# A hybrid decoder trunk on one core: k and three quarters of the gate's operand turned by VectorE in 32x32 blocks that their stores put in place

## The chip, the cores and the metric

One Trainium2 chip, one of its cores. The metric is the device time of one execution in microseconds (us), lower is better. Times of the kernel before are the median of 3 runs; the profile is of one execution more. In the profile PE is TensorE (matmuls), PEld its weight loads, DVE is VectorE, ACT is ScalarE, POOL is GpSimd, and SP is SyncE, whose queue issues almost all DMAs.

## The reference, cut to what matters

One layer of a decoder trunk on 1024 tokens of width 1024, in float32. A combined projection gives, among others, q, k, v, decay gates, and the inputs of a gated short convolution. Branch A is gated linear attention in 4 heads (key width 128, value width 256). Two branches are merged, projected, and added to x; then comes a gate on the sum:

```python
k_in = k * jnp.exp(-b)
k_dec = k * jnp.exp(b_last - b)
a = jnp.where(causal, jnp.einsum('nbhid,nbhjd->nbhij', q_in, k_in), 0.0)
...
def step(state, xs):
    q_n, k_n, v_n, d_n = xs
    o_n = jnp.einsum('bhcd,bhdv->bhcv', q_n, state)
    state = d_n[..., None] * state + jnp.einsum('bhcd,bhcv->bhdv', k_n, v_n)
...
x = x + jnp.einsum('bsd,de->bse', merged, w_out[i])
ple_gate = jax.nn.sigmoid(jnp.einsum('bsd,de->bse', rms_norm(x, norm_ple_g[i]), w_ple_gate[i]))
x = x + ple_gate * jnp.einsum('bsq,qd->bsd', p[i], w_ple_proj[i])
```

Two operands matter here. The state update multiplies k_dec, with time on the partitions, by v; k is made with its 128 key channels on the partitions, so it has to be turned. The gate's product needs x (after the sum) with channels on the partitions; the sum is made with tokens on the partitions, so it has to be turned too.

## The kernel before, in words

**Products.** Every float32 operand is split into a high and a low part of a faster type (`split`: ACT copies the high part, DVE subtracts), and a product is three matmuls, hi by hi, hi by lo and lo by hi (`mm3`). Large products are cut in quarters in Strassen's manner: seven products (k = 0 to 6) of 512x512 by 512x256 or the like instead of eight. A `Cell` is one such product's column block; its seven products run on up to three banks of PSUM, X, V and Y, each product as 12 matmuls of 512 columns. `Cell.run` holds the order: products 2, 4 and 6 all accumulate into Y, and what stands in Y after 2 and after 4 is read by ACT or DVE before the next goes on. The split operand blocks lie in a ring of 8 (`RING`), so an operand can be split up to some seven products ahead, and raw blocks are loaded further ahead (`run_groups`).

**Stages by time in the span.** Start, position embedding and first gate products (to 72 us); v (to 148); z_a (to 234); q and k (234 to 310); the convolution's inputs (to 615); attention woven between the merge gates' products (615 to 746); y_c and y_a (774 to 926); out (926 to about 1008), in four cells out0 to out3 of 256 tokens each, run in pairs; the gate, four cells gt0 to gt3, gt0 and gt1 as a pair and gt2 and gt3 in an order of their own (`CLOSE`), to the end. Cells out0 to out3 and gt0 to gt3 are the groups 0 to 3.

**k.** `k_cons` takes each of 8 k tiles (4 heads, 2 halves of the sequence; 128 channels by 512 times), multiplies it by decays into `kk` (128 x 4 x 256: in each of 4 blocks of times, 128 columns for the scores and 128 for the state), and stores the 256 columns with one DMA into columns 384 to 640 of a row block of the DRAM tensor `qkd`. In attention (`attend`), 32 steps (4 heads, 8 blocks of 128 times) load such rows as `qkl` (128 x 640). In `step_a` PE makes the scores and transposes the last 128 columns of `qkl` into PSUM, `read_a` splits that transpose into `keh` and `kel`, and in the next step PE multiplies it by v (`step_s`). The last block of each head has no state to update, so 28 steps have the transpose. All matmuls of a step are one bundle, which PE runs without other work between.

**The gate's operand.** In `make_out`, a finished tile of x (128 tokens x 512 columns; 4 groups, 2 row blocks i, 2 halves j: 16 tiles) is handed to `finish`, which stores it, weaves in a `flip` two ticks later, and squares it for the norm. `flip` transposes four 128x128 pieces on PE into one PSUM tile `pt_g`, ACT copies that into `gr` (3 buffers), and one DMA stores it into `gd`. The gate cells load their raw blocks from `gd` (`gt0raw` to `gt3raw`); a group's loads are free to start once its four flips have been emitted.

**The order of the work** is not written by hand. Every call is noted in a `Flow`, which keeps dependencies by blocks of `GRAIN` columns of a buffer, gives each operation a cost, works out due times back from the end (`set_dues`), and then orders all engines' instructions with a model of the engines and of the DMA pipe (`put_in_order`). The main products of PE keep their program order; PE's transposes and attention bundles are side work that the planner puts between them. The instructions are emitted in that order, and each engine runs its own in order. A DMA's size for the planner is its bytes, 4 for each element.

Since one line of code (line 520) emits everything, the profile tells instructions apart by the names of their tiles, and the buffer numbers are left out.

Of the kernel before, what the change touches and what calls it, by code (L numbers as in the profile page):

```python
# [9 lines left out]
F32 = mybir.dt.float32  # L10
# [6 lines left out]
P = 128  # L17
# [25 lines left out]


PE, DVE, ACT, POOL, SP = range(5)
GRAIN = 64
TABLE = {AF.Exp: 1, AF.Ln: 2, AF.Sigmoid: 3}


class View:  # L50
# [81 lines left out]
    def place(self):  # L132
        real = self.buf.get()
        if self.dtype != self.buf.dtype:
            real = real.bitcast(self.dtype)
        a, b = self.rows
        return bass.AP(tensor=real.tensor, offset=real.offset + a * self.buf.size + self.off,
                       ap=[[self.buf.size, b - a]] + [[s, n] for s, n in self.dims])


class Buffer:
# [105 lines left out]
class Flow:  # L247
# [12 lines left out]
    def note(self, engine, op, call, args, kw):  # L260
        views = [a for a in args if isinstance(a, View) or hasattr(a, "ap")]
        views += [a for k, a in kw.items() if k not in ("out", "accum_out") and (isinstance(a, View) or hasattr(a, "ap"))]
        outs, ins = ([kw["out"]], views) if "out" in kw else (views[:1], views[1:])
        if kw.get("accum_out") is not None:
            outs.append(kw["accum_out"])
        o = Op()
        o.n, o.engine, o.call, o.args, o.kw = len(self.ops), engine, call, args, kw
        o.side, o.table, o.bytes, o.bufs, o.hurry = self.side, 0, 0, [], self.hurry
        label = lambda v: v.buf.name if isinstance(v, View) else "in"
        o.name = f"{label(outs[0])}<-{','.join(label(v) for v in ins)}"  # L270
        shape = outs[0].shape
        n = 1
        for d in shape[1:]:
            n *= d
        o.lat = 0.15
        if op == "dma_start":
            o.cost, o.bytes = 0.4, shape[0] * n * 4
            o.lat = 2.0 + o.bytes / 250e3
        elif engine == PE:
            o.cost, o.lat = n / 2400 + 0.0134, 0.22  # L280
            if op == "transpose" or args[1].dtype == F32:
                o.cost = 0.11 if op == "transpose" else 0.22
            elif args[1].shape[0] < P:
                o.cost = 0.42
        elif engine == DVE:
            psum = any(isinstance(v, View) and v.buf.pool.name == "ps" for v in outs + ins)
            o.cost = 0.07 + n * (0.00055 if op in ("tensor_scalar", "tensor_copy") and not psum else 0.00104)
            if op in ("scalar_tensor_tensor", "tensor_scalar"):
                o.cost += 0.06
            if op == "tensor_tensor_scan":  # L290
                o.cost = 0.05 + n * 0.0021
        elif engine == ACT:
            o.cost = 0.10 + n * 0.000833 + (0.1 if "accum_out" in kw else 0.0) + (0.08 if len(ins) > 1 else 0.0)
            o.table = TABLE.get(args[2] if len(args) > 2 else None, 0)
        elif engine == POOL:
            o.cost = 0.1 + n * 0.001 if op == "memset" else 0.35 + 0.25 * n
        preds = {}

        def behind(p):
            if p is not None and p != o.n:  # L300
                q = self.ops[p]
                lat = q.lat
                if q.engine == engine and not q.bytes:
                    lat = 0.0 if engine == PE else 0.08
                preds[p] = max(preds.get(p, 0.0), lat)

        for v in ins:
            if isinstance(v, View):
                for b in v.blocks():
                    e = v.buf.memory.setdefault(b, [None, []])  # L310
                    behind(e[0])
                    e[1].append(o.n)
        for v in outs:
            if isinstance(v, View):
                for b in v.blocks():
                    e = v.buf.memory.setdefault(b, [None, []])
                    for p in [e[0]] + e[1]:
                        behind(p)
                    e[0], e[1] = o.n, []
                if engine == PE:  # L320
                    behind(v.buf.group)
                    v.buf.group = o.n
                for pool in v.buf.pool.instead:
                    for old in pool.buffers:
                        for p in old.users:
                            behind(p)
        for v in outs + ins:
            if isinstance(v, View) and v.buf not in o.bufs:
                if v.buf.index is None:
                    v.buf.index = len(v.buf.tag.buffers)  # L330
                    v.buf.tag.buffers.append(v.buf)
                o.bufs.append(v.buf)
                v.buf.users.append(o.n)
        o.preds, o.succs = preds, []
        for p in preds:
            self.ops[p].succs.append(o.n)
        self.ops.append(o)
        if engine == PE and not o.side:
            self.main.append(o)
        if self.bundle is not None and engine == PE:  # L340
            self.bundle.append(o)
# [195 lines left out]
def kernel(  # L537
# [56 lines left out]
    def dram(name, *shape):  # L594
        return dr.tile([P, *shape], F32, name=name)
# [11 lines left out]
    mcd = [[dram(f"mcd{k}_{i}", HALF) for i in range(2)] for k in range(8)]  # L607
    md = [dram(f"md{i}", 2, 2, 2, 4, P) for i in range(2)]
    x2d = [dram(f"x2d{b}", D) for b in range(8)]
    gd = [[dram(f"gd{p}_{q}", 2, 4, P) for q in range(2)] for p in range(4)]  # L610
    wtd = [[dram(f"wtd{w}_{n}", 4, 512) for n in range(4 + 3 * w)] for w in range(2)]

    load = nc.sync.dma_start
# [693 lines left out]
    with phase("qk", [ph["za"]]) as qp:  # L1307
# [35 lines left out]
        def k_cons(hp):  # L1343

            def cons(i, j, src):
                h = 2 * hp + j
                nm = f"{h}_{i}"
                c4 = get_c(h, i, "k")
                kk = qp.tile([P, NP, 4, CH], F32, tag="kk", name=f"kk{nm}", bufs=2)
                dc = dcs[:, h, i]  # L1350
                tt(kk[:, :, 0:4:3, :], c4, c4[:, :, :, CH - 1:CH].to_broadcast([P, NP, 2, CH]), op=ALU.subtract)
                ex(kk[:, :, 0:4:3, :], kk[:, :, 0:4:3, :], 1.0)
                ex(kk[:, :, 1, :], c4[:, :, 1, :], 1.0)
                k4 = src.rearrange("p (n c t) -> p n c t", c=2, t=CH)
                tt(kk[:, :, 0, :], k4[:, :, 0, :], kk[:, :, 0, :], op=ALU.mult)
                tt(kk[:, :, 1:4:2, :], k4[:, :, 1:2, :].to_broadcast([P, NP, 2, CH]), kk[:, :, 1:4:2, :],
                   op=ALU.mult)
                tt(kk[:, :, 2, :], kk[:, :, 0, :], dc[:, :, 1:2].to_broadcast([P, NP, CH]), op=ALU.mult)
                store(qkd[h][i][:, :, 3 * P:5 * P], kk.rearrange("p n s t -> p n (s t)"))
            return cons  # L1360

        for hp in range(2):
# [82 lines left out]
    def attend(hp, ap, every):  # L1445
# [21 lines left out]
        def step_a(it, X):  # L1467
            pr, h = its[it]
            qk = f(ins[it][0])
            mm(X[:, 0:P], qk[:, 3 * P:4 * P], qk[:, 2 * P:3 * P], start=True, stop=True)  # L1470
            if pr < 2 * NP - 1:
                transpose(X[:, P:2 * P], qk[:, 4 * P:5 * P])

        def read_a(it, X):
            pr, h = its[it]
            nm = f"{h}_{pr}"
            a = aTf[it % 2]
            nc.vector.copy_predicated(a, trim, X[:, 0:P])
            ke = None
            if pr < 2 * NP - 1:  # L1480
                ke = (ap.tile([P, P], F32R, tag="keh", name=f"keh{nm}", bufs=2),
                      ap.tile([P, P], F32R, tag="kel", name=f"kel{nm}", bufs=2))
                split(*ke, X[:, P:2 * P])
            aT = (ap.tile([P, P], F32R, tag="aTh", name=f"aTh{nm}", bufs=2),
                  ap.tile([P, P], F32R, tag="aTl", name=f"aTl{nm}", bufs=2))
            split(*aT, a)
            scores[it] = aT, ke
# [178 lines left out]
    with phase("late", [ph["sw"], ep]) as lp:  # L1666
        flipped, rgate, both = set(), {}, [None, None]

        def make_out(p, cell):
# [16 lines left out]
                    ms.append(sm.tile([P, 2], F32, tag="ms2", name=f"ms2_{p}_{i}", bufs=4))  # L1686

            def flip(i, j):
                pt = pso.tile([P, 4, P], F32, tag="o", name=f"pt_g{p}_{i}_{j}", bufs=2)
                for k in range(4):  # L1690
                    transpose(pt[:, k, :], xt[i][j][:, k * P:(k + 1) * P])
                g = lp.tile([P, 4, P], F32, tag="gr", name=f"gr{p}_{i}_{j}", bufs=3)
                nc.scalar.copy(g, pt)
                store(gd[p][j][:, i], g)
                yield 1
                flipped.add((p, i, j))

# [21 lines left out]

        for p in range(4):  # L1720
            make_out(p, outs[p])
        gts = [Cell(f"gt{p}", "A", [gd[p][n // 2][:, n % 2] for n in range(4)], gres, None) for p in range(4)]
        for p, c in enumerate(gts):
            c.ready = lambda k, p=p: {(p, i, j) for i in range(2) for j in range(2)} <= flipped
        with phase("sw4", lp.instead, lp) as pool:
# [183 lines left out]
```

## Time and profile before

| what | before |
|---|---|
| median of 3 runs | 1095.49 us (1095.38 to 1095.55) |
| the profiled execution's own time | 1095.63 us |
| its span, first to last instruction | 1093.8 us |
| mean granted clock of PE | 0.999 |
| DMA | 241.18 MB, 220 GB/s over the span |

A row of a group gives line, engine, operation, out<-in, shapes, how many; then, behind the bar, busy us in all and mean ns of one; then the engine's idle time just before them and what ended it. A row of a tile's view gives shortest, median and longest ns, and the first and last start in us. A row of the chain or of the timeline gives start, duration, engine, and what. PE's durations reach from the start of a matmul to its end, and matmuls overlap: the slot that one takes is the distance between starts. A DMA row on SPq is the time that SP needs to issue it, not the transfer.

### The profile page before, as it was taken

Reading aid. Unit: us, or ns where it says so; the run is one execution under the profiler, and the core shown is the slowest. Engines: PE = TensorE matmul, PEld = TensorE weight load, DVE = VectorE, ACT = ScalarE, POOL = GpSimd, SP = SyncE. Lnnn points to the kernel's source line nnn. Section 1 sums busy time; section 2 is a strip of 40 time slices with the busy share of each in tenths; the row PEclk is TensorE's granted clock in tenths of the full one; section 3 lists DMA queues with packets and bytes.
Section 4 is the critical chain, followed back from the end, with each engine's and each line's share of the span. In section 5 each row is a group of like instructions: output and inputs, shape, how many; then the busy total and the mean of one; then the engine's idle time right before and its main releaser. Section 6 shows DMA issues by size and latency. Waiting matters only on the chain.

```text
span 1093.8 us, 15337 instructions
## 1 busy us (share of the span) xinstructions
PE 1086.0 (99%) x5042; PEld 905.4 (83%) x5042; DVE 853.7 (78%) x1391; ACT 600.4 (55%) x1115; POOL 56.8 (5%) x117
## 2 busy tenths in 40 slices
PE   9999999999999999999999999999999999999997
PEld 7888888888888888888888888888888888888886
DVE  6996477879878869748649687776999889959586
ACT  5864447876543454343334376766735445468554
POOL 0000000000000000000000022220000000001021
PEclk9999999999999999999999999999999999999999
DMA  9986463358876595212212699988594888889762
GB/s 338 338 270 208 163 201 114 108 182 256 248 235 237 191 298 190 97 53 68 87 59 76 218 312 325 344 261 283 191 340 162 308 265 286 298 303 321 262 221 101
DMA packets 157599, 241.18 MB, mean 220 GB/s; under 512 B 13520, under 2 KB 68432, under 8 KB 157520
## 3 DMA queue, kind: packets, MB, share of 16 engines
q1 hardware_dynamic: 157088, 239.75, 65.7%
q8 instruction: 39, 0.64, 0.2%
q10 hardware_dynamic: 432, 0.46, 0.1%
q14 instruction: 40, 0.33, 0.1%
HBM read 159.55 MB, written 80.61 MB: 220 GB/s over the span
## 4 chain that ended last, share of the span: by engine, by line
PE 99%; ACT 0%; DVE 0%; issue 0%; POOL 0%; POOLq 0%; ACTq 0%
PE vacc L520 7%; PE op L520 3%; PE pe L520 2%; PE X L520 2%; PE gc1Y L520 1%; PE ga3Y L520 1%; PE ga2Y L520 1%; PE gc0Y L520 1%; PE ga1Y L520 1%; PE ga0Y L520 1%; PE out1Y L520 1%; PE out3Y L520 1%; PE out0Y L520 1%; PE out2Y L520 1%; PE za2Y L520 1%; PE za0Y L520 1%
## 5 line engine op out<-in xcount | busy, mean ns | idle before, releaser
L520 ACT ACT_TABLE_LOAD x18 | 23.1, 1283 | 1.9 <-PEq L1898 1.6
L520 ACT ACTIVATE junk<-x 128x512 bf16<-128x512 f32 (+1 forms) x29 | 17.8, 613 | 8.2 <-DVE x L520 8.0
L520 DVE TENSOR_TENSOR wt<-wt 128x512 f32<-128x512 f32 x32 | 21.7, 686 | 0.6 <-DMA wtd<-wt 0.4
L520 POOL TENSOR_TENSOR or<-or,mhalf 128x1 f32<-128x1 f32 x32 | 20.5, 642 | 2.7
L520 DVE SCALAR_TENSOR_TENSOR u<-t,vec,u 128x1024 f32<-128x1024 f32 x16 | 20.4, 1277 | 0.0
L520 POOL MEMSET t<- 128x2 f32 x8 | 0.8, 100 | 377.6 <-DVE u L520 194.8
L520 ACT ACTIVATE og<-op,or 128x256 f32<-128x256 f32 x32 | 15.1, 471 | 7.7 <-POOL or L520 7.6
L520 DVE COPY_PREDICATED aT<-trim,X 128x128 f32<-128x128 int32 x32 | 9.6, 300 | 11.2 <-PE X L520 11.1
L520 POOL TENSOR_SCALAR rg<-ms 128x1 f32<-128x1 f32 x8 | 4.8, 596 | 259.7 <-ACT junk L520 259.7
L520 POOL TENSOR_SCALAR or<-oms 128x1 f32<-128x1 f32 x32 | 9.7, 303 | 124.6 <-ACT junk L520 124.5
L520 PE MATMUL op<-vl,aTh 128*128 128x256 f32 x64 | 15.2, 318 | 0.0
L520 PE MATMUL op<-Sh,qkl 128*128 128x256 f32 x56 | 14.6, 283 | 0.0
L520 DVE TENSOR_TENSOR szl<-op,szl 128x256 f32<-128x256 f32 x32 | 13.5, 422 | 1.3 <-PE op L520 0.7
L520 ACT CAST aTh<-aT 128x128 fp32r<-128x128 f32 x32 | 9.5, 297 | 8.3 <-DVE aT L520 7.9
L520 ACT ACTIVATE junk<-op 128x256 bf16<-128x256 f32 x32 | 12.3, 384 | 2.3 <-DVE szl L520 1.4
L520 PE MATMUL pe<-wpehi,pThi 128*128 128x512 f32 (+1 forms) x36 | 13.0, 383 | 0.0
L520 PE MATMUL pe<-wpehi,pTlo 128*128 128x512 f32 (+1 forms) x36 | 12.9, 376 | 0.0
L520 PE MATMUL pe<-wpelo,pThi 128*128 128x512 f32 (+1 forms) x36 | 12.7, 372 | 0.0
L520 PEld LDWEIGHTS X<-vl,keh 128*128 128x128 f32 x56 | 10.5, 188 | 2.4
L520 PE MATMUL X<-qkl 128*128 128x128 f32 x64 | 12.3, 273 | 0.0
L520 PE MATMUL op<-ident,og 128*128 128x128 f32 x64 | 12.3, 272 | 0.0
L520 DVE TENSOR_TENSOR Sl<-S,Sh 128x256 fp32r<-128x256 f32 x28 | 11.7, 418 | 0.3 <-ACT Sh L520 0.2
(3251 smaller groups left out, 4157.6 us busy)
## 6 DMA issues: line engine op xcount, KB each, us to landing
wtd<-wt SPq DMA_DIRECT2D x44, 256.0 KB, 3.8
qkl<-qkd SPq DMA_DIRECT2D x32, 320.0 KB, 5.2
wt<-in_wb_dram SPq DMA_DIRECT2D x8, 1024.0 KB, 6.7
vl<-vd SPq DMA_DIRECT2D x32, 256.0 KB, 4.9
vraw<-in_wb_dram SPq DMA_DIRECT2D x28, 256.0 KB, 4.2
wgq<-wtd SPq DMA_DIRECT2D x14, 512.0 KB, 5.7
uq<-ud SPq DMA_DIRECT2D x10, 512.0 KB, 5.9
oq<-od SPq DMA_DIRECT2D x10, 512.0 KB, 6.9
```

What stands on the lines that cost most here:

```text
L520: o.call(*[place(a) for a in o.args], **{k: place(a) for k, a in o.kw.items()})
```

## The change

The transposes of k and of 12 of the 16 tiles of the gate's operand leave PE. VectorE's transpose turns each 32x32 block in place, not the whole 128x128 tile, so block (a, b) of the result stands at (a, b) and has to go to (b, a). The store does that: the 32 partitions of block row a go, with one DMA, to 32 columns of all 128 rows of the DRAM tensor, in runs of 32 elements (128 bytes). `Blocks` is a view that describes such a destination for the planner and for the DMA. Four such DMAs store one tile of 128x512.

In `k_cons` the score columns are stored as before, now by themselves, and the 128 state columns of each time block are turned into `kT` (from the pool `ev`, 3 buffers) and stored by four block stores. In attention PE no longer transposes, and `read_a` splits the loaded columns directly. In `flip`, groups 2 and 3 and row block 0 of groups 0 and 1 are turned by VectorE; row block 1 of groups 0 and 1 (four tiles) still goes over PE and ACT. `gd` becomes two DRAM tensors where it was one. The planner counts 10 bytes for each element of a block store, and its grain is 32 columns for every buffer.

```diff
-GRAIN = 64
+GRAIN = 32
...
+class Blocks(View):
+    def __init__(self, plain, s):
+        (step, n), _ = plain.dims
+        off = plain.off + 32 * s
+        super().__init__(plain.buf, (0, 32), off, [(step, n), (32 * plain.buf.size, 4), (1, 32)], plain.dtype)
+        self.columns = View(plain.buf, plain.rows, off, [(step, n), (1, 32)], plain.dtype)
+
+    def blocks(self):
+        return self.columns.blocks()
...
-            o.cost, o.bytes = 0.4, shape[0] * n * 4
+            o.cost, o.bytes = 0.4, shape[0] * n * (10 if isinstance(outs[0], Blocks) else 4)
...
-    gd = [[dram(f"gd{p}_{q}", 2, 4, P) for q in range(2)] for p in range(4)]
+    gd = [[[dram(f"gd{p}_{q}_{i}", 4, P) for i in range(2)] for q in range(2)] for p in range(4)]
...
-                store(qkd[h][i][:, :, 3 * P:5 * P], kk.rearrange("p n s t -> p n (s t)"))
+                kT = ev(f"kT{nm}").rearrange("p (n t) -> p n t", n=NP)
+                kf = kk.rearrange("p n s t -> p n (s t)")
+                nc.vector.transpose(kT, kf[:, :, P:2 * P])
+                store(qkd[h][i][:, :, 3 * P:4 * P], kf[:, :, 0:P])
+                for b in range(4):
+                    store(Blocks(qkd[h][i][:, :, 4 * P:5 * P], b), kT[32 * b:32 * b + 32].rearrange("p n (b t) -> p n b t", b=4))
...
-            if pr < 2 * NP - 1:
-                transpose(X[:, P:2 * P], qk[:, 4 * P:5 * P])
...
-                split(*ke, X[:, P:2 * P])
+                split(*ke, f(ins[it][0])[:, 4 * P:5 * P])
...
-                pt = pso.tile([P, 4, P], F32, tag="o", name=f"pt_g{p}_{i}_{j}", bufs=2)
-                for k in range(4):
-                    transpose(pt[:, k, :], xt[i][j][:, k * P:(k + 1) * P])
                 g = lp.tile([P, 4, P], F32, tag="gr", name=f"gr{p}_{i}_{j}", bufs=3)
-                nc.scalar.copy(g, pt)
-                store(gd[p][j][:, i], g)
+                if p >= 2 or i == 0:
+                    nc.vector.transpose(g.rearrange("p k t -> p (k t)"), xt[i][j])
+                    for b in range(4):
+                        store(Blocks(gd[p][j][i], b), g[32 * b:32 * b + 32].rearrange("p k (q t) -> p k q t", q=4))
+                else:
+                    pt = pso.tile([P, 4, P], F32, tag="o", name=f"pt_g{p}_{i}_{j}", bufs=2)
+                    for k in range(4):
+                        transpose(pt[:, k, :], xt[i][j][:, k * P:(k + 1) * P])
+                    nc.scalar.copy(g, pt)
+                    store(gd[p][j][i], g)
...
-        gts = [Cell(f"gt{p}", "A", [gd[p][n // 2][:, n % 2] for n in range(4)], gres, None) for p in range(4)]
+        gts = [Cell(f"gt{p}", "A", [gd[p][n // 2][n % 2] for n in range(4)], gres, None) for p in range(4)]
```

## The prediction, made before the changed kernel was run

> **What bounds the kernel now.** I read the page first: span and engines, then the chain that ended last, then what TensorE (PE) waited for.
>
> ```profile
> span 1093.8 us, 15337 instructions
> PE 1086.0 (99%) x5042; PEld 905.4 (83%) x5042; DVE 853.7 (78%) x1391; ACT 600.4 (55%) x1115; POOL 56.8 (5%) x117
> ...
> PE 99%; ACT 0%; DVE 0%; issue 0%; POOL 0%; POOLq 0%; ACTq 0%
> ```
>
> ```profile
> PE warm L520 <- PEq L1898: 0.8, 1, 0.8
> ```
>
> PE is busy for 99% of the span, the chain is 99% PE, and the list of PE's waits holds this one line. A busy PE need not be a fast one, so I looked at the pieces of the chain:
>
> ```profile
> 264.32 2.72 PE k0Y L520 x12
> 267.04 2.72 PE k0V L520 x12
> 269.76 2.72 PE k0Y L520 x12
> ```
>
> Twelve 512-column matmuls take 2.72 us, 0.227 each, and the next dozen starts where the last one ended. The kernel is PE's queue laid end to end; whatever leaves that queue shortens the run by its slot, as long as nobody is late with operands. The profiled execution took 1095.63 us, 1.8 more than its span; the median of the runs is 1095.49, so the same sum holds for both to 0.14 us.
>
> **What leaves PE.** The change takes out one transpose in each of 28 attention steps, and four in each of 12 flips (the turning of a tile for the gate; 16 flips now, of which groups 0 and 1 keep four). 28 + 48 = 76 transposes.
>
> ```profile
> L520 PE MATMUL X<-ident,qkl 128*128 128x128 f32 x28 | 7.6, 273 | 0.0
> L520 PE MATMUL pt_g<-ident,x 128*128 128x128 f32 x48 | 7.2, 272 | 0.0
> ```
>
> The 273 ns is the time from start to end of one; matmuls overlap, so the price is the slot between starts. One attention step with the transpose, then a later one without (the last pair has none):
>
> ```profile
> 729.96 0.40 PE L520 MATMUL X<-vl,keh 128*128 128x256 f32 x2
> ...
> 730.54 0.27 PE L520 MATMUL X<-ident,qkl 128*128 128x128 f32 x1
> ...
> 730.89 0.28 PE L520 MATMUL op<-vl,aTl 128*128 128x256 f32 x1
> ...
> 733.89 0.40 PE L520 MATMUL X<-vl,keh 128*128 128x256 f32 x2
> ...
> 734.71 0.29 PE L520 MATMUL op<-vl,aTl 128*128 128x256 f32 x1
> ```
>
> 730.89 - 729.96 = 0.93 against 734.71 - 733.89 = 0.82: the transpose costs 0.11 us, and 28 cost 3.1. A flip:
>
> ```profile
> 960.90 0.39 PE L520 MATMUL out0Y<-wo6lo,out0hi 128*128 128x512 f32 x1
> 961.14 0.60 PE L520 MATMUL pt_g<-ident,x2r 128*128 128x128 f32 x4
> 961.49 0.48 PE L520 MATMUL out0Y<-wo6hi,out0lo 128*128 128x512 f32 x1
> 961.81 0.39 PE L520 MATMUL out0Y<-wo6hi,out0hi 128*128 128x512 f32 x1
> ```
>
> 961.81 - 960.90 = 0.91 holds two big matmuls (2 x 0.227 = 0.45) and the four transposes: 0.45. Twelve flips free 5.4 us. Sum on PE: 3.1 + 5.4 = 8.5 us; one digit of rounding in each difference leaves 8.0 to 9.0. So 1095.63 - 8.5 = 1087.1.
>
> The Trainium skill ("TensorE: Matmul & The Clock Gate", Part 4: PE-mode transpose) gives about 275 ns for a transpose in a kernel. The trace agrees as to a single duration, not as to the slot of 0.11; by 275 the sum would be 20.9 us and 1074.7, and I give that no chance, since the starts are in the rows above.
>
> **What VectorE (DVE) gets.** Twenty transposes of 128x512: one in each of 8 k tiles, 12 flips. None is in the trace. Neighbours:
>
> ```profile
> L520 DVE TENSOR_TENSOR wt<-wt 128x512 f32<-128x512 f32 x32 | 21.7, 686 | 0.6 <-DMA wtd<-wt 0.4
> L520 DVE TENSOR_TENSOR_SCAN c<-smask,t 128x512 f32<-128x512 f32 x8 | 9.7, 1216 | 0.0
> L520 DVE TENSOR_SCALAR u<-t,vec 128x1024 f32<-128x1024 f32 x8 | 5.9, 747 | 0.0
> ```
>
> Lowest 0.37 (half of the 747 for twice the columns), highest 1.22; I take 0.69, the plain pass over this shape. 20 x 0.69 = 13.8 us, off PE. Its cover, by stage:
>
> ```profile
> 250.00:275.00 25.00, 25.00 (x112) 20.71 (x111) 24.63 (x53) 15.75 (x34) 0.00 (x0) 1.00 0.94 282
> 275.00:300.00 25.00, 25.00 (x112) 20.67 (x111) 22.04 (x45) 14.92 (x32) 0.00 (x0) 1.00 0.81 247
> 300.00:325.00 25.00, 25.00 (x112) 20.71 (x111) 18.44 (x33) 10.46 (x21) 0.20 (x2) 1.00 0.68 219
> 955.00:1020.00 65.00, 65.00 (x319) 53.94 (x318) 45.95 (x62) 44.54 (x80) 8.90 (x14) 1.00 0.89 318
> ```
>
> The columns are PE, PEld, DVE, ACT and POOL busy, then clock, DMA share and GB/s. The k tiles are made between 264 and 317 us: DVE has 75 - 65.1 = 9.9 us free in 250 to 325, and gets 8 x 0.69 = 5.5 (9.8 at the upper price). It is full for the first 25 us, so its queue will run behind; what waits for it is next:
>
> ```profile
> L520 DVE TENSOR_TENSOR k1lo<-k1raw,k1hi x3: 678/681/691, 273.4 to 287.2; 128x512 fp32r<-128x512 f32 x3
> ...
> L520 PE MATMUL k1X<-h0hi,k1lo x4: 389/389/389, 291.8 to 293.9; 128*128 128x512 f32 x4
> ```
>
> Even there an operand is split 18 us ahead of its matmul: the cover. The flips add 8.3 us to 45.95 of 65. The split of the turned k now reads SBUF and waits for the load instead of PE, at like prices; nobody on the path waits for it. ScalarE (ACT) loses 12 copies, worth nothing, as it bounds nothing.
>
> **What the SP queue gets.** A block store has 512 runs of 128 bytes and is issued four times a tile. Issues of 512 runs:
>
> ```profile
> L520 SPq DMA_DIRECT2D qkd<-qdh x8: 513/525/590, 251.7 to 303.4; - x8
> ...
> DMA to landing us min/median/max: 2.6/3.2/5.4
> ```
>
> ```profile
> L520 SPq DMA_DIRECT2D gd<-gr x16: 319/320/1095, 959.0 to 1018.2; - x16
> ```
>
> At 0.525 each, k adds 8 x 4 x 0.525 = 16.8 us of SP between 266 and 320, and a flip 4 x 0.525 - 0.32 = 1.8, or 21 us between 957 and 1020 (0.59, the longest, makes that 24.5). Behind them wait the loads of raw weight blocks, needed 18 us later. New waits: SP waits for the DVE transpose as it now waits for ACT's copy; a DVE transpose waits for its buffer until all four stores of an earlier one have landed, and behind it wait the additions that free PSUM banks.
>
> **What the DMA engines get.** The trace shows no 128-byte data packets. I price them by a line through two rows, the whole run and a stretch of small packets (160 to 220 us):
>
> ```profile
> q1 hardware_dynamic: 157088, 239.75, 65.7%
> ```
>
> ```profile
> q1 hardware_dynamic: 8233, 7.11, 38.1%
> ```
>
> 0.657 x 16 x 1093.8 / 157088 = 73.2 ns for 1526 bytes; 0.381 x 16 x 60 / 8233 = 44.4 ns for 864. Slope 0.0435 ns per byte, 6.8 fixed: 128 bytes come to 12.4 ns. The lower end is 6.8, the upper is 44.4 itself; I take 12.4, since both rows lie on it. A turned tile of 2048 packets then takes 2048 x 12.4 / 16 = 1.59 us of all engines, against 128 x 95.9 / 16 = 0.77: 12 flips add 9.8 us. A k tile's store was 512 packets of 1024 bytes (51.3 ns each, 1.64 us) and becomes 1.59 for the blocks and 512 packets of 512 bytes (29.1 ns each, 0.93 us): 0.88 more, 7 us in a stage whose share is 0.68 to 0.94. The late stage is the tight one (955 to 1030, then 1030 to 1050):
>
> ```profile
> q1 hardware_dynamic: 10825, 24.35, 90.3%
> ```
>
> ```profile
> q1 hardware_dynamic: 978, 1.78, 28.1%
> ```
>
> ```profile
> L520 DVE TENSOR_TENSOR gt2lo<-gt2raw,gt2hi x3: 678/689/692, 1029.3 to 1051.1; 128x512 fp32r<-128x512 f32 x3
> ...
> L520 PE MATMUL gt2X<-wg0hi,gt2lo x4: 389/389/389, 1048.2 to 1050.2; 128*128 128x512 f32 x4
> ```
>
> Free before group 2's operand is needed, which now is 1048.2 - 8.5 = 1039.7: 9.7% of 75 = 7.3 us, and 9.7 us at 72% = 7.0; 14.3 in all. The eight turned tiles of groups 0 to 2 add 8 x 0.82 = 6.6. It fits.
>
> **Rivals.**
>
> *Packets cost more.* From (14.3 / 8 + 0.77) x 16 / 2048 = 20.0 ns a packet the gate's operand is late, and PE stalls 8 x 2048 / 16 = 1.02 us per ns above it. At twice the line's price, 24.8 ns, it loses 4.9: 1092.0. For it: the share of 90% and no packet so short in the trace; against it: the two rows. The Trainium skill says, in "DMA: Bandwidth & Descriptors", Specifications, that under 512 bytes the engines read, modify and write; doubling is an estimate of mine for that. No run here shows it yet. Chance 0.07.
>
> *The same mechanism to the slower side.* From 20.0 + 8.5 / 1.02 = 28.3 ns the stall at gt2 eats the whole gain; at 44.4 ns it is 25 us and the kernel ends at 1112. Chance 0.03.
>
> *The four stores of a tile wait for one another*, because they interleave in one DRAM tensor. Each wait is a landing, 3.2 us or more, on the queue that carries all loads: three in each of 12 flips put 115 us on SP within 63. It decides as soon as the waits exist: 115 - 63 = 52 us over, 1139 or more. Against it:
>
> ```profile
> 251.70 0.51 SPq L520 DMA_DIRECT2D qkd<-qdh  x1
> 252.32 0.57 SPq L520 DMA_DIRECT2D ck<-cd  x1
> 252.97 0.52 SPq L520 DMA_DIRECT2D qkd<-qdl  x1
> ```
>
> Two interleaved stores into one tensor, 1.3 us apart, when one needs at least 2.6 to land. Chance 0.03.
>
> *Small PE gaps.* Between two products on one bank PE leaves 2.72 us (the k0V row above) for DVE or ACT to read it; a transpose of 0.69 that starts just ahead of that read, behind a queue that is full or a buffer not yet free, makes PE wait. The order is also planned anew, with a finer grain of dependencies for every tile. Half of the 20 transposes costing 0.25 each is 2.5: 1089.6. For it: 24.63 of 25. Against: with that very queue PE had no gap. Chance 0.13, of which 0.02 lose it all.
>
> **How the numbers follow.** My forecast has 0.74 and its own range is 1086.6 (9.0 freed) to 1088.5. It is 1087.1. Of the span 7.8 us have no busy PE; a new order may close 1 us of it: low end 1085.7. The upper end takes in the gaps of 2.5 and up to 4: 1091.0. Outside lie mostly the dear packets and the waiting stores. About 0.2%, 2.2 us, is what can be told from no change. Faster: 0.74 + 0.11 + 0.04 of the 0.07 = 0.89. Same: 0.02 + 0.03 = 0.05. Slower: 0.03 + 0.03 = 0.06.
>
> **What would show it.** Right: X<-ident,qkl gone, 16 transposes left in pt_g, an attention step short by 0.11, PE's waits still next to empty, PE busy near 1077.5, and DVE transposes near 0.69. Wrong: a new PE wait on gt2 or gt3 lo or hi with DVE or ACT waiting for gt2raw (packets); SP issues of qkd or gd a landing apart (stores); PE waits of a few tenths on k0, k1 or out banks (gaps). A longer DVE transpose alone changes nothing unless it passes 1.2.

## The result, and the profile after

The changed kernel takes 1089.51 us (median of 4 runs, 1089.00 to 1089.94) against 1095.52 for the kernel before beside it; the ratio is 0.9944, 95% interval 0.9932 to 0.9955. That is 6.0 us, where 8.5 were forecast: faster, and inside the range, but above the 1088.5 at which the forecast's own range ended. The profiled execution took 1089.63, 6.0 less than the one before. Four executions of three kernels further on ran at a far lower granted clock (0.56 to 0.85, 1197 to 1836 us) and are left out of the medians below.

The page of the changed kernel, the same three lines as before (its lines of code moved from L520 to L534):

```profile
span 1087.8 us, 15258 instructions
...
PE 1078.1 (99%) x4966; PEld 897.3 (82%) x4966; DVE 864.0 (79%) x1411; ACT 595.6 (55%) x1104; POOL 59.3 (5%) x117
...
PE 97%; DMA 1%; SPq 1%; DVE 0%; issue 0%; ACT 0%; POOL 0%; POOLq 0%; DVEq 0%; ACTq 0%
```

PE's busy time fell by 7.9 us, near the 8.5 of the sum. The chain of work that ended last, 99% PE before, now has pieces of DMA and of SP's queue in it: that is where to look. PE's waits, one line before, are four:

```profile
PE warm L534 <- PEq L1920: 0.8, 1, 0.8
PE pe L534 <- DVE wpelo L534: 0.7, 1, 0.7
PE gt0Y L534 <- DVE gt0s L534: 0.7, 1, 0.7
PE gt1Y L534 <- DVE gt1s L534: 0.5, 1, 0.5
```

I compared the start of each main matmul in the two traces. The changed kernel is 0.6 us behind at 8 us, 0.8 behind from the z_a stage on, 2.25 ahead after attention (so 3.1 were gained there), 7.8 ahead after the flips (5.5 more), 6.9 to 7.05 ahead in gt0Y's product 6 and 6.0 after gt1Y's. So the 8.5 were all gained, 0.8 were lost before attention, and 1.7 to 1.8 in the gate, at the two places that the list of waits names.

What PE lost and kept, in an attention step (PE's timeline) and in the flips (PE's groups):

```profile
727.83 0.40 PE L534 MATMUL X<-vl,keh 128*128 128x256 f32 x2
...
728.65 0.29 PE L534 MATMUL op<-vl,aTl 128*128 128x256 f32 x1
```

```profile
L534 PE MATMUL pt_g<-ident,x2r x8: 270/272/273, 960.9 to 963.1; 128*128 128x128 f32 x8
...
L534 PE MATMUL pt_g<-ident,x x8: 270/272/273, 965.7 to 968.1; 128*128 128x128 f32 x8
```

The step takes 0.82 where it took 0.93, and 16 transposes of the gate's operand are left.

**How the gate lost 1.7 us.** VectorE's timeline in the changed kernel, with idle time and its releaser in brackets:

```profile
1022.58 0.71 DVE L534 STREAM_TRANSPOSE gr<-x 128x512 f32<-128x512 f32 x1 [3.03 <-DMA gd<-gr]
...
1030.74 0.69 DVE L534 TENSOR_TENSOR pe<-gt1u,pe 128x512 f32<-128x512 f32 x1 [0.79 <-ACT gt1u L534]
1033.87 0.69 DVE L534 TENSOR_TENSOR x<-x,pe 128x512 f32<-128x512 f32 x1 [2.44 <-DMA x<-x2d]
1034.48 0.69 DVE L534 TENSOR_TENSOR gt0s<-gt0Y,gt0s 128x512 f32<-128x512 f32 x1
```

DVE waits 2.44 us for a load of x. The addition right behind it reads PE's bank gt0Y, and PE has one other product (2.72 us) to run before it needs that bank again. The wait uses that time up and 0.7 more. The longer wait of 3.03 above it, for a buffer, costs PE nothing: no bank waits at that time. Why the load was late shows SP's queue:

```profile
1026.71 2.65 SPq L534 DMA_DIRECT2D gd<-gr  x4
1029.40 0.63 SPq L534 DMA_DIRECT2D x<-x2d  x1
1030.13 2.61 SPq L534 DMA_DIRECT2D gd<-gr  x4
1032.84 0.84 SPq L534 DMA_DIRECT2D pe<-ped  x1
1033.72 0.43 SPq L534 DMA_DIRECT2D x<-x2d  x1
1034.19 1.39 SPq L534 DMA_DIRECT2D gt2raw<-gd  x3
```

Each group of four block stores holds SP for 2.65 us, and the loads stand between and behind them. From 1005 to 1036 us SP's rows add up to 26.5 of 31 us; in the kernel before to 12.1. The chain of the changed kernel says the same for gt1Y:

```profile
1032.11 0.63 SPq L534
...
1032.84 3.78 DMA pe<-ped
...
1036.71 0.72 DVE pe L534
...
1037.45 0.69 DVE x L534
1038.15 0.61 DVE gt1s L534
...
1038.80 3.06 PE gt1Y L534 x12
```

Read upwards: PE's product waited for gt1s, that for the addition to x, that for the one to pe, that for the load of pe, and that load for SP, which was issuing block stores.

### The profile page after: what moved, and what is told of

Same layout as the page of the kernel before. It is cut to its first block, busy times and chain, and to the rows that moved or that the text cites. A ratio compares the mean times of both kernels' runs of the same rounds, so it can differ in the third digit from the quotient of the medians.

```text
span 1087.8 us, 15258 instructions
## 1 busy us (share of the span) xinstructions
PE 1078.1 (99%) x4966; PEld 897.3 (82%) x4966; DVE 864.0 (79%) x1411; ACT 595.6 (55%) x1104; POOL 59.3 (5%) x117
## 4 chain that ended last, share of the span: by engine, by line
PE 97%; DMA 1%; SPq 1%; DVE 0%; issue 0%; ACT 0%; POOL 0%; POOLq 0%; DVEq 0%; ACTq 0%
PE vacc L534 7%; PE op L534 3%; PE pe L534 2%; PE X L534 2%; PE ga2Y L534 1%; PE gc1Y L534 1%; PE ga3Y L534 1%; PE gc0Y L534 1%; PE ga0Y L534 1%; PE ga1Y L534 1%; PE gt2Y L534 1%; PE za2Y L534 1%; PE out1Y L534 1%; PE za0Y L534 1%; PE za1Y L534 1%; PE out3Y L534 1%
## 5 line engine op out<-in xcount | busy, mean ns | idle before, releaser
L534 ACT ACTIVATE junk<-x 128x512 bf16<-128x512 f32 (+1 forms) x29 | 17.8, 614 | 15.4 <-DVE x L534 13.1
L534 DVE TENSOR_TENSOR wt<-wt 128x512 f32<-128x512 f32 x32 | 21.8, 688 | 0.3
L534 POOL MEMSET t<- 128x2 f32 x8 | 0.8, 99 | 377.9 <-DVE u L534 194.9
L534 DVE SCALAR_TENSOR_TENSOR u<-t,vec,u 128x1024 f32<-128x1024 f32 x16 | 20.5, 1283 | 0.0
L534 POOL TENSOR_TENSOR or<-or,mhalf 128x1 f32<-128x1 f32 x32 | 20.0, 625 | 2.7
L534 POOL TENSOR_SCALAR rg<-ms 128x1 f32<-128x1 f32 x8 | 5.4, 675 | 254.8 <-ACT junk L534 254.8
L534 ACT ACTIVATE og<-op,or 128x256 f32<-128x256 f32 x32 | 15.1, 471 | 5.6 <-POOL or L534 5.6
L534 DVE TENSOR_TENSOR szl<-op,szl 128x256 f32<-128x256 f32 x32 | 13.5, 422 | 3.9 <-PE op L534 3.1
L534 DVE COPY_PREDICATED aT<-trim,X 128x128 f32<-128x128 int32 x32 | 9.6, 301 | 8.3 <-PE X L534 8.3
L534 POOL TENSOR_SCALAR or<-oms 128x1 f32<-128x1 f32 x32 | 9.3, 292 | 122.6 <-ACT junk L534 122.6
L534 PE MATMUL op<-vl,aTh 128*128 128x256 f32 x64 | 15.4, 321 | 0.0
L534 PE MATMUL op<-Sh,qkl 128*128 128x256 f32 x56 | 14.5, 281 | 0.0
L534 DVE TENSOR_TENSOR x<-x,pe 128x512 f32<-128x512 f32 (+1 forms) x17 | 11.1, 656 | 3.4 <-DMA x<-x2d 3.1
L534 ACT ACTIVATE junk<-op 128x256 bf16<-128x256 f32 x32 | 12.2, 381 | 2.3 <-DVE szl L534 2.0
L534 PE MATMUL pe<-wpelo,pThi 128*128 128x512 f32 (+1 forms) x36 | 12.7, 371 | 0.7 <-DVE wpelo L534 0.7
L534 PE MATMUL pe<-wpehi,pThi 128*128 128x512 f32 (+1 forms) x36 | 13.1, 384 | 0.0
L534 PE MATMUL pe<-wpehi,pTlo 128*128 128x512 f32 (+1 forms) x36 | 12.7, 373 | 0.0
L534 PEld LDWEIGHTS X<-vl,keh 128*128 128x128 f32 x56 | 10.5, 188 | 2.4
L534 PE MATMUL X<-qkl 128*128 128x128 f32 x64 | 12.3, 273 | 0.0
L534 ACT CAST aTh<-aT 128x128 fp32r<-128x128 f32 x32 | 9.5, 295 | 5.2 <-DVE aT L534 5.0
L534 ACT CAST Sh<-S 128x256 fp32r<-128x256 f32 x28 | 11.3, 403 | 1.8 <-PE op L534 0.5
```

What stands on the lines that cost most here:

```text
L534: o.call(*[place(a) for a in o.args], **{k: place(a) for k, a in o.kw.items()})
```

## The experiments

Theories, by the letters of the expectations: A, the block stores hold SP's queue, and the loads behind them come late (A2: by their number alone); B, VectorE's transposes wait for a buffer `gr`, with additions behind them; C, VectorE's own added work; P, the 128-byte packets fill the DMA engines. The experiments change the changed kernel, where nothing else is said.

**The k part alone.** All flips back on PE.

```diff
-                if p >= 2 or i == 0:
+                if False:
```

> Only k is turned by VectorE; all 16 flips are back on TensorE. The changed kernel lost about 2.4 us of the 8.5 that left TensorE: 0.6 at the start, 1.7 around the last products of gt0 and gt1. Theory A (SP: a block store takes 0.66 us to issue, so in the out stage the queue falls behind and loads come late, with VectorE's additions behind them): 28 x 0.11 = 3.1 us less than before, 1092.4, and no TensorE wait on gt0s or gt1s. Theory B (the three gr buffers, held until four stores have landed) and theory C (VectorE's added work in the out stage) say the same of this run. Theory K (k's turning costs something too, in the q and k stage): above 1092.9. Theory D (the 0.6 at the start is the chance of when the first loads land): the wait on wpelo is 0 or 0.6, independent of the change.

1093.84 against 1095.7, ratio 0.9983 (0.9974 to 0.9992). That is above the 1092.9 from which the expectation puts a cost down to k's own stage (theory K), and the trace bears only a little of it out. PE loses 0.3 us at the start, 0.2 in z_a and 0.2 in the k stage, gains the 3.1 in attention, and is 2.35 ahead from there to its end; no bank waits. The last store then lands 0.7 later, which leaves 1.6. In the changed kernel the k stage lost nothing. So the k part costs 0.2 us in its own stage at the most.

**The flips alone.** `k_cons`, `step_a` and `read_a` as in the kernel before.

```diff
-                kT = ev(f"kT{nm}").rearrange("p (n t) -> p n t", n=NP)
...
+                store(qkd[h][i][:, :, 3 * P:5 * P], kk.rearrange("p n s t -> p n (s t)"))
...
+            if pr < 2 * NP - 1:
+                transpose(X[:, P:2 * P], qk[:, 4 * P:5 * P])
```

> Only 12 flips are turned by VectorE; k goes over TensorE as before. Theories A, B and C: 5.4 us leave TensorE and about 1.7 come back as waits on gt0s and gt1s: 1095.5 - 3.7 = 1091.8. Theory K: 1090.5, without these waits.

1092.49, ratio 0.9970 (0.9960 to 0.9981), where 1091.8 was expected. PE's waits in the profiled execution, which with 1094.53 was the slowest of the seven:

```profile
PE gt2V L534 <- ACT gt3hi L534: 1.1, 1, 1.1
PE out2Y L534 <- DVE x L534: 1.0, 1, 1.0
...
PE gt1Y L534 <- DVE gt1s L534: 0.6, 1, 0.6
```

These waits give back 2.7 us of the 5.4 in that execution; by the medians 2.2 are given back. Two of the three waits are not those of the changed kernel, though all lie between the out stage and the gate. The loss belongs to the flips.

**One plain store for a turned tile.** The blocks stay where VectorE leaves them, so that part of the result isn't the reference's.

```diff
-                    for b in range(4):
-                        store(Blocks(gd[p][j][i], b), g[32 * b:32 * b + 32].rearrange("p k (q t) -> p k q t", q=4))
+                    store(gd[p][j][i], g)
```

> VectorE turns k and the 12 tiles, but each turned tile of the gate's operand goes out with one plain store, with its blocks left where they are; so the gate's operand is not the transpose, and only the time is read. Theories A and B: no TensorE wait on gt0s or gt1s, 1087.1 to 1087.8. Theory C (VectorE's added work): the waits stay, 1089.5.

1087.3, ratio 0.9922 (0.9909 to 0.9936): the forecast's number. VectorE turns the same tiles, and no bank waits. C falls: the loss comes with the four block stores. A and B are both left, as the expectation said.

**The planner told of the true issue time.** 0.66 us of SP for a block store, not 0.4.

```diff
-            o.cost, o.bytes = 0.4, shape[0] * n * (10 if isinstance(outs[0], Blocks) else 4)
+            o.cost, o.bytes = (0.66, shape[0] * n * 10) if isinstance(outs[0], Blocks) else (0.4, shape[0] * n * 4)
```

> The same work, but the planner counts 0.66 us of SP for the issue of a block store, where it counted 0.4. Theory A: the planner puts the gate's and x's loads where SP can really issue them, the waits on gt0s and gt1s shrink or go: 1087.1 to 1088.3. Theory B: the buffers are as scarce, 1089.5 within 0.5.

1095.53, ratio 0.9998 (0.9989 to 1.0007). A clear miss: the whole gain is gone. The profiled execution was the fastest, 1094.04; its waits:

```profile
PE gt1Y L534 <- DVE gt1s L534: 3.5, 1, 3.5
PE gt2X L534 <- ACT gt2Y L534: 1.0, 1, 1.0
PE pe L534 <- DVE wpelo L534: 0.8, 1, 0.8
```

The new order put twelve block stores in a row (7.97 us of SP from 1023.94) ahead of gt2raw's loads; DVE waited 4.1 us for these with gt1s behind. A truer number for one operation did not give a better order; why the planner chose this one isn't shown.

**Four stores of long runs.** Each of the four takes 32 whole rows (runs of 2 KB), unturned; `Part` is a view that says so to the planner. The order of the instructions is the changed kernel's on every engine and in SP's queue, so this is the cleanest comparison of all. Part of the result isn't the reference's.

```diff
-                        store(Blocks(gd[p][j][i], b), g[32 * b:32 * b + 32].rearrange("p k (q t) -> p k q t", q=4))
+                        store(Part(gd[p][j][i], b), g[32 * b:32 * b + 32])
```

> The same plan and the same four stores for each of the 12 turned tiles, but each goes to 32 whole rows of 2 KB instead of 512 runs of 128 bytes; the blocks stay where they are, so the gate's operand is not the transpose and only the time is read. Plain_store has shown that it is the stores, not VectorE's added work. Theory A (SP's issue time goes with the number of runs: 0.66 us for 512): a store costs SP 0.32 to 0.38, a tile 1.4 instead of 2.65, and the waits on gt0s and gt1s are gone: 1087.1 to 1088. Theory A2 (four issues are too many, whatever is in them): the waits stay, 1089.5.

1087.25, ratio 0.9926 (0.9912 to 0.9939), no bank waits. A2 falls. What is left is that the short runs take SP longer, or the packets. SP's issues to `gd`, in this kernel and in the changed one:

```profile
L541 SPq DMA_DIRECT2D gd<-gr x52: 302/419/961, 950.6 to 1025.2; - x52
```

```profile
L534 SPq DMA_DIRECT2D gd<-gr x52: 376/627/2117, 951.1 to 1032.1; - x52
```

0.42 against 0.63 us an issue (1.7 and 2.5 a tile), and the last flip's stores are issued 7 us earlier. The load of x that VectorE waited for in the changed kernel was issued at 1029.40; here it is

```profile
1022.69 0.43 SPq L541 DMA_DIRECT2D x<-x2d  x1
```

and the time from issue to landing of such loads between 1005 and 1036 us (the last number, in us) is this in the kernel before, in this one and in the changed one:

```profile
x<-x2d SPq DMA_DIRECT2D x3, 512.0 KB, 5.5
x<-x2d SPq DMA_DIRECT2D x4, 512.0 KB, 5.2
x<-x2d SPq DMA_DIRECT2D x4, 512.0 KB, 4.4
```

Among the short packets a load lands no later after its issue than among long ones. It was issued 6.7 us later. That decides between A and P: the loads were late because SP issued them late.

**Eight stores of long runs.** To part A from P by a run as well: SP as busy as with block stores, packets as few as with a plain store (unturned too).

```diff
-                    for b in range(4):
-                        store(Blocks(gd[p][j][i], b), g[32 * b:32 * b + 32].rearrange("p k (q t) -> p k q t", q=4))
+                    for b in range(8):
+                        store(Part(gd[p][j][i], b), g[16 * b:16 * b + 16])
```

> The changed kernel with each tile that VectorE turns for the gate stored by eight DMAs of 16 whole rows (2 KB runs) instead of four block stores, the turned blocks left where they are; so that part of the gate's result is not the reference's, and only its time is read. The planner counts 0.2 us for each of the eight, and the same bytes and dependencies in halves, so that its plan stays near. At about 0.32 us an issue SP spends 2.6 us a tile, as with the block stores (2.65), but the tile is 128 packets and not 2048 (0.77 us of the DMA engines and not 1.6). Theory A, SP's issue time is what delays the x and gt2raw loads: the waits on gt0Y and gt1Y come back, 1089.0 to 1089.8. Theory P, the time of the 128-byte packets on the DMA engines does: no waits on the gt banks, 1087.0 to 1087.6, as with long runs in four stores.

1099.55, ratio 1.0031 (1.0017 to 1.0044): far past what either theory gave. An issue took 0.42 us, not 0.32, so a tile held SP for 8 x 0.418 = 3.3 us.

```profile
PE out2Y L545 <- DVE x L545: 4.8, 1, 4.8
PE gt0Y L545 <- DVE gt0s L545: 3.1, 1, 3.1
PE gt2V L545 <- ACT gt3hi L545: 0.9, 1, 0.9
```

The DMA engines meanwhile, from 1005 to 1035 us, in this kernel and then in the changed one (packets, MB, share of the 16 engines):

```profile
q1 hardware_dynamic: 3376, 6.50, 66.7%
```

```profile
q1 hardware_dynamic: 16356, 6.01, 86.6%
```

With a fifth of the packets and the DMA engines idle for a third of the time the same bank waits, and for longer: P isn't needed for the loss. The kernel before had 86.7% in this stretch and no wait, which speaks against P as well. The wait on gt0Y hangs again on a load of x behind stores of turned tiles (VectorE waits 3.9 us for it); how the 4.8 on out2Y comes about was not followed to its start, and VectorE also waits 5.7 us for a buffer (4.6 in the changed kernel), so A and B aren't parted here. VectorE and ScalarE run in the changed kernel's order, so a new plan for them isn't the cause. Nor is the size of the loss a price for an issue, because PE's clock adds to it. After the wait of 4.8 us the slots of PE's matmuls are 0.43 us, where they are 0.227 elsewhere, and the granted clock (the number after POOL's) is 0.50:

```profile
1001.90 0.63 PE L545 MATMUL out2Y<-wo6lo,out2hi 128*128 128x512 f32 x1
1002.33 0.63 PE L545 MATMUL out2Y<-wo6hi,out2lo 128*128 128x512 f32 x1
```

```profile
1001.30:1004.30 3.00, 2.96 (x7) 2.41 (x8) 3.00 (x5) 1.23 (x3) 0.10 (x1) 0.50 0.89 210
```

Six to eight matmuls are so slow, which adds about 1.5 us. The profiles show 3.4 us of this clock after each of PE's six waits of 2.5 us or more in the out and gate stages of the kernels here (two in this one, one each with the true issue time and with ScalarE's issues, two with all 16 tiles), and none after the waits of 2.0 us or less.

**Half of the block stores issued by ScalarE.**

```diff
-                        store(Blocks(gd[p][j][i], b), g[32 * b:32 * b + 32].rearrange("p k (q t) -> p k q t", q=4))
+                        (nc.scalar.dma_start if b % 2 else store)(Blocks(gd[p][j][i], b), g[32 * b:32 * b + 32].rearrange("p k (q t) -> p k q t", q=4))
```

> Two of the four block stores of each turned tile of the gate's operand are issued by ScalarE instead of SP; the packets are the same. Theory A (SP's issue time): SP has 12 x 1.3 = 16 us less to issue, loads come in time, the waits on gt0s and gt1s go: 1087.1 to 1088.3. Theory P (the packets, 1.6 us of all DMA engines for each tile, make loads late, whoever issues them): the waits stay, 1089.5. A slower result means that ScalarE now waits for the turned tile with something queued behind.

1091.16, ratio 0.9960 (0.9946 to 0.9973), with a wait of 3.0 us on gt0Y. SP's rows are down to 14 of 31 us, but ScalarE runs its own queue in order:

```profile
1031.46 3.37 ACTq L534 DMA_DIRECT2D gd<-gr  x2
1034.88 0.72 ACT L534 ACTIVATE gt1u<-gt1u,rg 128x512 f32<-128x512 f32 x1 [4.80 <-DMA gfin<-in_gbc_dram]
```

The 3.37 us reach from the start of the first issue to the end of the second. An issue takes 0.58; for 2.2 us between them ScalarE waits, by the profile for the landing of a load of gfin that SP issued, and why a store should wait for that isn't shown. The gate's gt1u stood behind, DVE waited for that, and gt0s stood behind DVE's wait. The stall moved to another queue with work behind it.

**Two buffers for a turned tile, not three.**

```diff
-                g = lp.tile([P, 4, P], F32, tag="gr", name=f"gr{p}_{i}_{j}", bufs=3)
+                g = lp.tile([P, 4, P], F32, tag="gr", name=f"gr{p}_{i}_{j}", bufs=2)
```

> Two gr buffers instead of three. Theory B (a transpose waits for a buffer, and the additions queue behind it): VectorE's waits for gr rise from 4.6 us to 9 or more, and TensorE's waits on gt0s and gt1s from 1.2 to 3 or more: 1091.5 or slower. Theory A alone: the same work on SP, 1089.5 within 0.7.

1088.13, ratio 0.9933 (0.9917 to 0.9948): not slower, and 1.4 us under the changed kernel, though the two intervals overlap. Neither theory gave this time. Nothing but 0.3 on out2Y and two waits of 0.8 in the first 9 us is left of PE's waits, although SP is as busy (28.2 of 31 us from 1005 to 1036, issues of 0.627). With a buffer less the planner orders transposes, stores and loads otherwise, and VectorE doesn't wait for gr at all, where it waited 4.6 us in the changed kernel. So the run doesn't put B to the test that was meant. What stands against B is the changed kernel's own trace: its wait of 3.03 us for a buffer cost PE nothing, and PE's two waits hang on loads. The run does show that a full queue alone doesn't make the loss; which load stands behind which stores decides whether PE pays.

**Other tiles for VectorE.** All eight of groups 0 and 1 and row block 0 of groups 2 and 3, twelve as before.

```diff
-                if p >= 2 or i == 0:
+                if p < 2 or i == 0:
```

> Again 12 flips on VectorE, but other ones: all eight of groups 0 and 1, whose operand is needed late, and only row block 0 of groups 2 and 3. TensorE does as much as in the changed kernel. Theories A and B: four turned tiles instead of eight in the stretch of 1005 to 1035 us, so SP falls less behind and the waits on gt0s and gt1s shrink to under 0.5: 1087.1 to 1088.3. If instead the eight early tiles crowd the wg operand's loads, new waits appear in out2 or out3.

1090.22, ratio 0.9955 (0.9943 to 0.9968). Waits of 0.5 to 0.9 at three other places (pt_g, gt2V, out2Y): the loss has moved, and it isn't smaller than in the changed kernel.

**The loads of x issued by GpSimd.** This takes the one late load out of SP's queue.

```diff
-                        load(xt[i], x2d[2 * p + i])
+                        nc.gpsimd.dma_start(xt[i], x2d[2 * p + i])
```

> The changed kernel with the eight loads of x for the gate's sum (x2d to x) issued by GpSimd instead of SP; all stores as in the changed kernel. Theory A, the x load stands in SP's queue behind block stores and VectorE's addition for product 6 stands behind that load: VectorE's wait of 2.4 us on x goes, PE's waits on gt0Y and gt1Y go, and the kernel gains the 1.2 to 1.7 us lost there: 1087.8 to 1088.4 (0.6 to 0.8 at the start stays or not). Theory P, the DMA engines are full of small packets: the load lands as late whoever issues it, 1089.2 to 1089.8. If GpSimd's own way of issuing is slow, x lands later still and gt0Y waits longer: over 1090.

1090.43, ratio 0.9958 (0.9945 to 0.9970).

```profile
PE gt2V L534 <- ACT gt2hi L534: 2.0, 1, 2.0
PE warm L534 <- PEq L1920: 0.8, 1, 0.8
PE gt2V L534 <- DVE gt2lo L534: 0.7, 1, 0.7
```

The step that A names holds: DVE doesn't wait for x, gt0Y and gt1Y are gone from the list, and PE is the full 8.5 us ahead until gt2V. Then the next load in SP's queue is the late one: gt2raw is issued from 1036.94 on, behind the block stores and the loads of pe, and PE waits 2.7. The cure of one wait only showed the next.

**The kernel before, replanned.** Nothing but its grain.

```diff
-GRAIN = 64
+GRAIN = 32
```

> The kernel before with nothing but the planner's grain at 32 columns instead of 64. If a new plan by itself costs PE a few tenths (the theory that any new order does), 1095.8 to 1096.5 with a wait or two of PE in the trace; if the grain does nothing, 1095.4 to 1095.7 and the list of PE's waits as before. The wait for the first loads at the start, 0.7 in the changed kernel and none in the kernel before, tells in either case whether it comes and goes with one and the same order.

1095.76 against 1095.42, ratio 1.0004 (0.9995 to 1.0013): no difference. Its profile has one new wait of PE, 0.8 us for wpelo at the start, with the same instructions in the same order there as in the kernel before, whose profile has none.

**All 16 tiles on VectorE, two buffers.** The step further that the good result invited.

```diff
-                g = lp.tile([P, 4, P], F32, tag="gr", name=f"gr{p}_{i}_{j}", bufs=3)
-                if p >= 2 or i == 0:
+                g = lp.tile([P, 4, P], F32, tag="gr", name=f"gr{p}_{i}_{j}", bufs=2)
+                if True:
```

> The changed kernel with two buffers for the turned tile, and all 16 flips on VectorE (the last four tiles leave PE too). Four flips at 0.45 us leave PE, 1.8 us. If the order with two buffers holds (no waits on the gt banks, 1088.1 with 12 flips), it is 1086.3. If SP's queue is what limits, four more tiles at 2.65 us of SP against 0.32 put 9.3 us more on SP between 950 and 1000, loads fall behind again, and the 1.8 are given back or more: 1088 to 1091, with waits of PE on out or gt banks.

1097.22, ratio 1.0014 (1.0005 to 1.0023): 1.8 us less on PE, and 9 slower than with 12 flips, past the 1091 that was expected at the worst. Two of its waits are followed by PE's slow matmuls. Its waits and its issues:

```profile
PE gt2V L534 <- ACT gt2hi L534: 2.8, 1, 2.8
PE out3V L534 <- DVE x L534: 2.5, 1, 2.5
PE gt0Y L534 <- DVE gt0s L534: 1.0, 1, 1.0
```

```profile
L534 SPq DMA_DIRECT2D gd<-gr x64: 569/628/3467, 950.3 to 1047.1; - x64
```

The last stores go out at 1047.1, 14 us later than with 12 flips and two buffers (1033.2).

Side by side, SP's time for the stores to `gd` (issues by median) and the result:

| kernel | SP for gd, us | time, us |
|---|---|---|
| one plain store | 16 x 0.320 = 5.1 | 1087.3 |
| four long stores | 52 x 0.419 = 21.8 | 1087.3 |
| two buffers | 52 x 0.627 = 32.6 | 1088.1 |
| the changed kernel | 52 x 0.627 = 32.6 | 1089.5 |
| other tiles | 52 x 0.628 = 32.7 | 1090.2 |
| x issued by GpSimd | 52 x 0.627 = 32.6 | 1090.4 |
| true issue time in the plan | 52 x 0.627 = 32.6 | 1095.5 |
| all 16, two buffers | 64 x 0.628 = 40.2 | 1097.2 |
| eight long stores | 100 x 0.418 = 41.8 | 1099.6 |

With up to 22 us on SP nothing was lost. At 32.6 the time depends on the order, from 1088.1 to 1095.5 with the same work, and at 40 neither of the two orders tried saved the gain.

## Why the prediction was right, and which step failed

**What leaves PE: right.** 3.1 and 5.5 us were gained where 3.1 and 5.4 were expected; the plain store shows the sum undisturbed. (The row of 48 transposes that the prediction shows is not the 48 that leave: tiles of the name x2r have 16 more, and of the 64 in all 16 stay.)

**VectorE: right.** The transposes, in the changed kernel:

```profile
L534 DVE STREAM_TRANSPOSE kT<-kk x8: 676/711/718, 268.0 to 319.4; 128x512 f32<-128x512 f32 x8
```

0.71 against 0.69, and turning them costs PE nothing (C).

**What the SP queue gets: the step that failed.** The prediction put it so: "Behind them wait the loads of raw weight blocks, needed 18 us later." That held in the k stage, where 32 issues of 0.624 went unnoticed, and not in the gate. The price of 0.525 was short by a fifth (0.627, so 48 issues are 30 us where 25 were counted), but the cover was the larger error. Behind the block stores of groups 2 and 3 stand loads of x, pe and gt2raw, which are needed a few us after their issue, and the 18 us were read from loads that had been issued by a queue with room. With the stores in it the second operand of group 2 was split 3.3 us ahead of its matmul (1041.55 and 1044.87), where the kernel before had 18.6; the first still had 18.9. SP's rows in that stretch (12.1 of 31 us) were not added up before the 21 us were laid on top, and the loads behind were not named one by one. The term left out measures 1.7 us in the profiled execution. With the 0.8 lost before attention it makes up, to 0.1, the 2.4 by which the time lies above 1087.1.

The Trainium skill ("Perfetto Trace Analysis", What "DMA-bound" means) counts a solid track of DMA issues on the issuing engine's sequencer as a limit of its own, beside the DMA engines. The traces agree in part: SP is issuing for 26.5 of 31 us in the changed kernel, and the loads issued there land no later after their issue than in the kernel before. But SP was as full with two buffers, and little was lost. The same page (DMA Optimizations) says that spreading the issues over several engines may help then. Here neither way was faster: ratios of 0.9960 with half of the block stores on ScalarE and 0.9958 with the loads of x on GpSimd, against 0.9944.

**What the DMA engines get: right.** It fits, as forecast: between 1005 and 1036 us the loads of x, pe and gt2raw landed a median of 4.4, 3.8 and 4.8 us after their issue, in the kernel before 5.5, 4.7 and 5.0. The line of the changed kernel's profile page,

```profile
q1 hardware_dynamic: 197600, 239.75, 68.3%
```

has 40512 packets more than before for the same bytes, and 0.683 x 16 x 1087.8 - 0.657 x 16 x 1093.8 = 389 us more of engine time: 9.6 ns for each added packet beside its bytes, where the line through two rows had 6.8. With the line's 5.6 for the bytes, a packet of 128 bytes comes to an estimated 15.2 ns, dearer than 12.4 and below the 20.0 from which the first rival begins. The doubling (24.8) that was estimated from the Trainium skill ("DMA: Bandwidth & Descriptors", Specifications) is not seen.

**The rivals.** The stores of a tile don't wait for one another: they go out 0.63 us apart. The small PE gaps gave 1089.6, and that is what came, but by another road: the wait was for a load, at gt0Y and gt1Y, and not for a buffer or a transpose ahead of a read, at k or out. That the number agrees is luck, and the range reached as far as 1091.0 because of this rival, so the time fell into it for a reason that the prediction did not have. "The order is also planned anew" was the part of it that held: two buffers, the true cost and the other tiles each moved the waits, by 1 to 6 us, with nearly the same work on SP.

**Open.** The 0.6 at the start is lost before any instruction differs; the order first does at 163 us. Of the thirteen profiles taken after the one before, four have no wait for wpelo and nine have 0.3 to 0.8; the replanned kernel before is among the nine, with an unchanged time. The wait isn't the loss, either: with two buffers it is 0.8, and PE isn't behind at 40 us. Whether the loss is chance or goes with the program wasn't settled. The other 0.2, in z_a, goes with the finer grain: the replanned kernel before loses it too. Nor is it known how the planner would have to price a DMA to find the order of the two buffers by design.

## What to carry to other kernels

Before work is moved to stores, add up what the issuing queue already does in that stretch, and list the loads that stand behind the new issues with the time at which each is needed: a lead measured while the queue had room says nothing about the lead once it is full. A small wait of one engine costs nothing until an instruction that frees a PSUM bank stands behind it in the same queue. A long wait of PE can cost more than its own length, so look at the clock after it. When one late load is cured, ask which is the next in the queue, since the loss here only moved.

## What the runs showed of the hardware

The time that SP needs for an issue follows the runs and their shape, not the bytes: 64 KB in 512 runs of 128 bytes from 32 partitions took 0.63 us, in 32 runs of 2 KB 0.42 in a busy queue, and 256 KB in 512 runs of 512 bytes 0.525 in the kernel before. The number of runs alone doesn't set it: 128 runs of 2 KB took 0.32 with one plain store for a tile. ScalarE took 0.58 for the same block store. VectorE turns 128x512 float32 in 32x32 blocks in 0.71 us, 0.02 more than a plain pass over it. After waits of 2.5 to 4.8 us in the out and gate stages PE's granted clock was 0.50 for 3.4 us and a 512-column matmul took a slot of 0.427 us; after waits of 2.0 us and less it stayed at 1.00 with slots of 0.227.
